# Two layers of a decoder trunk on one core: a ring of weight slots that gives the oldest, up panels with their pairs at other steps, and a third pair in two of them

## The chip, the core and the metric

The kernel runs on one core of a Trainium2 chip. The metric is the device time of one execution in microseconds. Weights come from HBM in every execution. TensorE (PE in the profile) multiplies, VectorE (DVE) and ScalarE (ACT) prepare its operands and take its results, SyncE (SP) and GpSimd (POOL) issue transfers.

## The reference

256 tokens of width 2048 pass through two layers: gated linear attention, then forgetting attention, each beside a cross attention into 256 memory tokens, and each followed by the same kind of channel mixer (FFN). All the change is in the FFN:

```python
def causal_dwconv(u, w, b):
    s_ = u.shape[1]
    up = jnp.pad(u, ((0, 0), (CONV_WIDTH - 1, 0), (0, 0)))
    return w[0] * up[:, 0:s_] + w[1] * up[:, 1:s_ + 1] + w[2] * up[:, 2:s_ + 2] + b

def conv_ffn(h, w_up, conv_w, conv_b, w_down):
    u = causal_dwconv(h @ w_up, conv_w, conv_b)
    a, val = split_cols(u, [FFN_HIDDEN, FFN_HIDDEN])
    return (jax.nn.silu(a) * val) @ w_down

# in each layer i, after the attention:
    h = rmsnorm(x, norm_ffn[i])
    x = x + conv_ffn(h, ffn_w_up[i], ffn_conv_w[i], ffn_conv_b[i], ffn_w_down[i])
```

FFN_HIDDEN is 5632, so w_up is 2048 x 11264 and w_down 5632 x 2048, all in float32.

## The kernel before

**Products.** A float32 operand is split into a high part in a rounded type and the low rest: `hi = cast(raw)` on ACT, `lo = raw - hi` on DVE. A product of two split operands is three products on PE: high with high, low with high, high with low. The activations `h` are split once. The weights are split as they come: one *unit* is 128 x 1024 elements (512 KB). SP loads it into a *raw slot* (L232), ACT casts it into a `whi` buffer (L242), DVE forms `wlo` (L243), and PE uses both (L421). There are five `whi` and five `wlo` buffers.

**The raw slots.** Five home slots (`RAWS`) serve the whole kernel. Each FFN adds two guests (the tile `raw2`) and drops them when it ends. `raw_slot` takes the next one by a counter modulo the number of slots. The guests' memory belonged to other tiles before: in both FFNs a load into a guest waits until the block `blk`, a transposed piece of the residual stream that the norm needs, has been written to its place in DRAM (`far`).

**Panels.** In each FFN 11 up panels of 16 units follow each other, numbered here 0 to 10 (`j // 4` in the code), with the parts of the down projection between them: panels 0 to 4, two down panels of 16 units, panels 5 to 7, two of 12 units, panels 8 to 10, and the last down panels. A *single* is one unit: 12 products of 512 columns. A *pair* is two units multiplied by a scheme with seven block products instead of eight (`pair_steps`): 21 products of 512 columns instead of 24. For it DVE forms differences of the two raw units in place (L446 to L449), there are four splits instead of two (w1 of half a unit, w2, w3, w4; L391 and L392), and the sums of the matching input blocks must be there (`usum`, made by `input_sums` and `token_sums`). w3 is cast from what L446 and L447 leave, w4 from what L448 and L449 leave. The products p1 to p7 and the singles go to eight PSUM banks; fast banks and slow banks change places from panel to panel (`flip`). When the last pair of a panel is done, `early` adds the banks p6, p7 and p5 on DVE (L1515 to L1518) into temporaries. When the last unit is done, `late` adds the banks p2, p4, p3 and x on DVE (L1524) and transposes the four results (L1475), which go through DRAM by POOL's transfers and come back for the convolution: taps on ACT (L1425), their sums (L1432), the gated product (L1445) and its split (L538), in DVE and ACT time of later panels.

**What sets the order.** A scheduler puts each engine's instructions into one queue at compile time, by the order of the code, priorities (`high_priority`) and `issue_after`; on the chip each queue runs in its order. The step at which a pair stands in a panel comes from `sums` and `ahead`: panels 0, 3 and 4 have one pair (units 6 and 7) at step 6; the panels of `MORE_IN` have two, units 6 and 7 at step 4 and units 11 and 12 at step 9. A step is one unit, so a pair takes two.

Of the kernel before, what the change touches and what calls it, by code (L numbers as in the profile page):

```python
# [34 lines left out]
SEVEN_UP = (6,)  # L35
# [2 lines left out]
MORE_IN = (1, 2, 5, 6, 7, 8, 9, 10)  # L38
SCRATCH = 4096
RAWS = 5  # L40


LEVELS = (64, 16, 4)
# [105 lines left out]
def _trunk(ctx: ExitStack, tc: tile.TileContext, xt, xtok, memt, wp, wgu, gns, gfin, cnv, par, msk, out):  # L149
# [36 lines left out]

    loads, casts, lows, ends, last_mm, sent = [], [], [], [], [], []
    home = rear.tile([P, RAWS * NUNIT], F32, name="raw")
    slots, taken = [home[:, i * NUNIT : (i + 1) * NUNIT] for i in range(RAWS)], [0]

    def raw_slot():

        taken[0] += 1
        return slots[taken[0] % len(slots)]
    scratch = [sm]
    parked = []

# [194 lines left out]
            lows.append(V.tensor_tensor(lo[:, :n], src, hi[:, :n].bitcast(F32), ALU.subtract))  # L392
        return hi, lo

    def pair_steps(units, src, sums, flip, pool, early, late, ahead=0):

        bank = {}
        fast, slow = ("p1", "p5", "p7", "p6"), ("p2", "p3", "p4", "x")
# [7 lines left out]
        plan = []  # L406
        at = 0
        while at < n:
            if at + ahead in sums:
                plan.append(at + ahead)  # L410
                at += 2
            else:
                plan.append(single.pop(0))
                at += 1
# [19 lines left out]
        for k in plan:  # L434
            if k in sums:
                with tc.high_priority(offset=AHEAD):
                    ra, rb = raw_slot(), raw_slot()
                    with tc.issue_after(loads[-1].ins):
                        for t, (off, _, w) in ((ra, units[k]), (rb, units[k + 1])):
                            loads.append(nc.sync.dma_start(t, wp[off : off + P * w].rearrange("(p n) -> p n", p=P)))  # L440
                st = [[sums[k][:, part, j, :] for part in range(2)] for j in (3, 0, 1, 2)]
                done = k == end[-1]
                w1 = split_more(ra[:, :512], 512)
                w2 = split_more(rb, 1024)
                with tc.high_priority(offset=AHEAD):
                    V.tensor_tensor(ra[:, :512], ra[:, 512:], ra[:, :512], ALU.subtract)  # L446
                    V.tensor_tensor(ra[:, 512:], rb[:, 512:], ra[:, 512:], ALU.subtract)  # L447
                    V.tensor_tensor(rb[:, 512:], rb[:, 512:], ra[:, :512], ALU.subtract)  # L448
                    summed = V.tensor_tensor(rb[:, :512], rb[:, :512], rb[:, 512:], ALU.subtract)  # L449
                three("p1", tok(k, 0), [t[:, :512] for t in w1], done)  # L450
                three("p2", tok(k + 1, 0), [t[:, :512] for t in w2])
                three("p3", st[3], [t[:, 512:] for t in w2])
                with tc.issue_after(summed.ins):
                    w3 = split_more(ra, 1024)
                three("p5", st[0], [t[:, :512] for t in w3], done)
                three("p7", st[2], [t[:, 512:] for t in w3], done)
                w4 = split_more(rb, 1024)
                three("p6", st[1], [t[:, 512:] for t in w4], done)
                last_mm.append(three("p4", tok(k + 1, 1), [t[:, :512] for t in w4]))
                if done:  # L460
                    with tc.issue_after(casts[-1].ins), tc.issue_after(lows[-1].ins):
                        early(bank)
                yield -1
                yield -1
                continue
            else:
                w = split_unit(units[k])
                last = k == n - 1
                steps = [(low, *place) for low in range(2) for place in places]
                if last:  # L470
                    steps.sort(key=lambda t: places.index(t[1:]))
                for low, name, b, h in steps:
                    for part in range(2 - low):
# [881 lines left out]
    def down_pair(l, p, f, src, sums, flip, pool, temps, then=None):  # L1355
# [17 lines left out]
            if then is not None:  # L1373
                then(f + h, b)

        return pair_steps(where["down", l, p, f], src, sums, flip, pool, early, late)

    def add_out(key, src, then=None, spare=None, last=None, first=0, hooks=None, late=1):

# [23 lines left out]
    def ffn(l, nx, h, m, ys, zs, landing, then, pool, temps, last=None, spare=None):  # L1403
        with tc.tile_pool(name=f"ffn{l}", bufs=1) as fp:
# [3 lines left out]
            up_sums = {k: held("usum", k) for k in (*SEVEN_UP, SEVEN_MORE)}  # L1408
            rooms = {i: held("dsum", i) for i in range(2)}
            guest = pool.tile([P, 2 * NUNIT], F32, name="raw2")  # L1410
            slots.extend(guest[:, i * NUNIT : (i + 1) * NUNIT] for i in range(2))
            cw = fp.tile([P, 4 * 88], F32, name="cw")
            nc.sync.dma_start(cw, cnv[l])
            taps = [fp.tile([P, 2, 2, T + i], F32, name=f"tap{i}") for i in range(3)]
# [41 lines left out]
            def input_sums(k):  # L1456

                r = fp.tile([P, 2, T], F32, name="cv", tag="cv")
                for s in range(2):
                    V.tensor_tensor(r[:, s, :], h[k + s][:, 0, :].bitcast(F32), h[k + s][:, 1, :].bitcast(F32), ALU.add)  # L1460
                token_sums(r, up_sums[k])


            def scale(b):
# [39 lines left out]
            def up_pair(j):  # L1504
# [17 lines left out]
                def late(b, h_, a):  # L1522
                    with tc.issue_after(turned_last[0].ins) if h_ and not b else nullcontext():
                        V.scalar_tensor_tensor(u[b, h_], a, scale(b), u[b, h_], ALU.mult, ALU.add)  # L1524
                    turns[h_](b, u[b, h_])

                return pair_steps(where["up", l, j], h, {k: up_sums[k] for k in (*SEVEN_UP, SEVEN_MORE)[: 1 + second]},
                                  count[2] % 2, pool, early, late, 2 * second)

            def first(k):  # L1530
                {2: lambda: nx.land(landing[0]), 3: nx.take, 8: nx.col,
# [7 lines left out]
                    tick(share if k >= 0 else 0.0)  # L1539

            def drive_up(j):
                drive(up_pair(j), 1.7 if j // 4 in MORE_IN else 1.45)

            for k in SEVEN_UP:
                input_sums(k)
# [50 lines left out]
            else:  # L1596
                hooks = {(2, 3): then.land, (2, 5): then.land, (2, 7): then.take, (3, 1): then.take, (3, 2): then.land,
                         (3, 5): then.take}
                for f, step, at in ((2, f2, 3), (3, f3, 0)):
                    for u in range(at, 8):  # L1600
                        step(u)
                        hooks.get((f, u), int)()
            del slots[RAWS:]

    def preparing(name, dst, pool, far, kept=None, tag="blk", queue=nc.sync):

# [204 lines left out]
```

## Time and profile before

| | |
|---|---|
| median of 3 runs | 2221.41 us (2220.82 to 2221.58) |
| the profiled execution | 2219.84 us |
| its span, first to last instruction | 2218.0 us |
| mean granted PE clock | 0.997 |
| PE, PEld, DVE, ACT busy | 99%, 83%, 82%, 65% of the span |
| second FFN's first product of L421 | 1502.39 us from the start |

PE is matrix multiplication, PEld its weight loads beside it, SPq the sequencer that issues transfers. A wait for several events is put down to the one that came last. An engine's waits matter where PE waits for them in the end. The rows shown below give start, length, engine, line, operation, written tile, read tiles and count, and in brackets how long the engine was idle ahead of it and what ended that.

### The profile page before, as it was taken

What the parts mean: (1) busy time and instruction counts of PE and PEld (TensorE: products, weight loads), DVE (VectorE), ACT (ScalarE), POOL (GpSimd) and SP (SyncE); (2) the same over time, 40 slices, a digit from 0 to 9 for tenths busy, and PEclk for the clock granted to TensorE, in tenths of its full rate; (3) what the DMA queues carried; (4) which work ended last, traced back from release to release, by engine and by line L of the source; (5) the groups of instructions that cost most, each with busy time, mean ns of one, the idle gap of its engine ahead of it and who ended that gap; (6) DMA issues with size and microseconds to landing.
All of it is one profiled execution on the core that took longest, in us unless ns stands there. A gap on an engine that the chain in (4) does not pass through costs nothing.

```text
span 2218.0 us, 30190 instructions
## 1 busy us (share of the span) xinstructions
PE 2196.9 (99%) x10285; PEld 1846.7 (83%) x10285; DVE 1828.6 (82%) x2715; ACT 1437.8 (65%) x2280; POOL 136.8 (6%) x257
## 2 busy tenths in 40 slices
PE   9999999999999999999999999999999999999998
PEld 7888888878888888888888998877888888888886
DVE  7768976679988889889987569668998888988996
ACT  6655655557887568647865555445788657765874
POOL 0000000001100000001010000000100000100000
PEclk9999999999999999999999999999999999999999
DMA  9766666776777667666877667666687667776683
GB/s 360 260 222 217 199 207 230 252 231 223 258 250 239 199 228 256 231 207 224 268 246 245 219 207 235 224 217 223 224 263 248 222 203 245 242 236 211 230 283 113
DMA packets 166291, 515.41 MB, mean 232 GB/s; under 512 B 20780, under 2 KB 42552, under 8 KB 166136
## 3 DMA queue, kind: packets, MB, share of 16 engines
q1 hardware_dynamic: 149064, 460.99, 63.2%
q0 software_dynamic: 16496, 51.71, 7.4%
q8 instruction: 80, 1.31, 0.2%
q10 hardware_dynamic: 576, 0.79, 0.1%
q14 instruction: 75, 0.61, 0.1%
HBM read 469.62 MB, written 43.79 MB: 231 GB/s over the span
## 4 chain that ended last, share of the span: by engine, by line
PE 96%; DVE 2%; ACT 1%; DMA 1%; issue 0%; SPq 0%; DVEq 0%; ACTq 0%
PE acc L421 29%; PE acc L347 26%; PE ps_s L421 15%; PE ps_o L421 7%; PE ps_t L421 7%; PE acc L273 3%; PE acc L318 3%; PE ps_s L347 2%; PE acc L377 2%; PE acc L271 1%; PE ps_s L1044 0%; DMA raw<-wp 0%; ACT whi L242 0%; PE ps_o L710 0%; PE ps_s L710 0%
## 5 line engine op out<-in xcount | busy, mean ns | idle before, releaser
L243 DVE TENSOR_TENSOR wlo<-raw,whi 128x1024 fp32r<-128x1024 f32 (+2 forms) x685 | 812.5, 1200 | 222.9 <-ACT whi L242 200.8
L242 ACT ACTIVATE whi<-raw 128x1024 fp32r<-128x1024 f32 (+2 forms) x685 | 704.3, 1045 | 347.8 <-PE acc L347 131.2
L347 PE MATMUL acc<-whi,B 128*128 128x512 f32 (+3 forms) x1248 | 290.9, 369 | 0.0
L391 ACT ACTIVATE whi<-raw 128x1024 fp32r<-128x1024 f32 (+1 forms) x184 | 173.7, 953 | 179.4 <-DVE raw L447 65.7
L347 PEld LDWEIGHTS acc<-whi,B 128*128 128x128 f32 x1248 | 226.8, 188 | 28.1
L392 DVE TENSOR_TENSOR wlo<-raw,whi 128x1024 fp32r<-128x1024 f32 (+1 forms) x184 | 198.3, 1084 | 26.8 <-ACT whi L391 23.8
L421 PE MATMUL acc<-whi,mix 128*128 128x512 f32 x746 | 191.7, 392 | 8.7 <-ACT whi L242 8.7
L421 PE MATMUL acc<-whi,B 128*128 128x512 f32 x720 | 186.9, 389 | 0.0
L421 PEld LDWEIGHTS acc<-whi,mix 128*128 128x128 f32 x746 | 141.2, 189 | 38.7 <-ACT whi L242 9.2
L347 PE MATMUL acc<-wlo,B 128*128 128x512 f32 (+3 forms) x624 | 159.1, 369 | 0.0
L421 PEld LDWEIGHTS acc<-whi,B 128*128 128x128 f32 x720 | 135.1, 188 | 28.5 <-ACT whi L242 0.5
L347 PEld LDWEIGHTS acc<-wlo,B 128*128 128x128 f32 x624 | 114.2, 188 | 14.6
L1425 ACT ACTIVATE tap<-yzu,cw 128x256 f32<-128x256 f32 x264 | 120.7, 534 | 5.4 <-DMA yzu<-far 5.4
L1425 ACT ACTIVATE tap<-fvt,cw 128x256 f32<-128x256 f32 x264 | 120.2, 530 | 3.1 <-DMA fvt<-far 3.1
L1432 DVE TENSOR_TENSOR tap<-tap,tap 128x1024 f32<-128x1024 f32 x88 | 106.7, 1213 | 9.0 <-ACT tap L1425 9.0
L421 PE MATMUL acc<-wlo,mix 128*128 128x512 f32 x373 | 105.0, 392 | 0.0
L421 PE MATMUL acc<-wlo,B 128*128 128x512 f32 x360 | 103.8, 389 | 0.0
L421 PE MATMUL ps_s<-whi,mix 128*128 128x512 f32 x374 | 103.8, 389 | 0.0
L421 PE MATMUL ps_s<-whi,B 128*128 128x512 f32 x324 | 89.9, 389 | 0.0
L421 PEld LDWEIGHTS acc<-wlo,mix 128*128 128x128 f32 x373 | 70.6, 189 | 14.8
L421 PEld LDWEIGHTS ps_s<-whi,mix 128*128 128x128 f32 x374 | 70.2, 188 | 14.6
L421 PEld LDWEIGHTS acc<-wlo,B 128*128 128x128 f32 x360 | 67.6, 188 | 14.0
(503 smaller groups left out, 3912.8 us busy)
## 6 DMA issues: line engine op xcount, KB each, us to landing
raw<-wp SPq DMA_DIRECT2D x741, 512.0 KB, 4.6
fvt<-far POOLq DMA_DIRECT2D x100, 128.0 KB, 5.2
raw<-wp SPq DMA_DIRECT2D x32, 384.0 KB, 3.4
far<-yu POOLq DMA_DIRECT2D x22, 512.0 KB, 3.0
far<-yzu POOLq DMA_DIRECT2D x22, 512.0 KB, 3.0
yzu<-far POOLq DMA_DIRECT2D x88, 128.0 KB, 4.8
raw<-wp SPq DMA_DIRECT2D x24, 388.0 KB, 3.5
x<-xtok SPq DMA_DIRECT2D x8, 512.0 KB, 7.0
```

What stands on the lines that cost most here:

```text
L242: casts.append(S.activation(hi[:, s], raw[:, s], AF.Copy))
L243: lows.append(V.tensor_tensor(lo[:, s], raw[:, s], hi[:, s].bitcast(F32), ALU.subtract))
L271: mm = TE.matmul(acc[p][c][:, :T], w[:, s], both[:, 0, :], start=False, stop=end and j == 3)
L273: mm = TE.matmul(acc[p][c], w[:, s], both, start=u == j == 0, stop=end and j == 3)
L318: mm = TE.matmul(acc[b][:, :n], src[kcs[j] - base][:, part, b * P : (b + 1) * P], w, start=u == 0 and low == part == j == 0, stop=u == end ...
L347: mm = TE.matmul(acc[b][:, :n], src[kc - base][:, part, b * P : (b + 1) * P], ready[low][:, j * room : j * room + n], start=i == low == pa ...
L377: mm = TE.matmul(acc[b][:, :n], src[kc - base][:, part, b * P : (b + 1) * P], w, start=i == low == part == j == 0, stop=i == end and low = ...
L391: casts.append(S.activation(hi[:, :n], src, AF.Copy))
L392: lows.append(V.tensor_tensor(lo[:, :n], src, hi[:, :n].bitcast(F32), ALU.subtract))
L421: r = TE.matmul(bank[name], x, w, start=name not in begun, stop=last)
L1425: S.activation(by_run(taps[i][:, s, c, i:]), zs[slot][:, :, 2 * c + s], AF.Copy if i else AF.Identity, bias=0.0 if i else w[3], scale=w[2 ...
L1432: V.tensor_tensor(taps[0], taps[0], taps[n][:, :, :, :T], ALU.add)
```

## The change

- The ring takes its oldest slot: `raw_slot` moves the first of the list to its end. The guests wait in `coming` and join the list's front at the first pair of the FFN; at the end of the FFN they are taken out.
- A table `UP_STEPS` tells at which step which pair stands. One pair: as before. Two pairs: steps 3 and 10 instead of 4 and 9. Three: steps 1, 6 and 11.
- Up panels 5 and 8 (`THIRD_IN`, the sixth and the ninth) have a third pair, units 13 and 14. The sums for it are made in that panel, after its first two steps, in the room of a `dsum` tile.
- `input_sums` issues behind the latest `lo` subtraction.

```diff
+UP_STEPS = ({6: 6}, {3: 6, 10: 11}, {1: 6, 6: 11, 11: 13})
+THIRD, THIRD_IN = 13, {5: 1, 8: 0}
...
-    slots, taken = [home[:, i * NUNIT : (i + 1) * NUNIT] for i in range(RAWS)], [0]
+    slots, coming = [home[:, i * NUNIT : (i + 1) * NUNIT] for i in range(RAWS)], []
...
-        taken[0] += 1
-        return slots[taken[0] % len(slots)]
+        slots.append(slots.pop(0))
+        return slots[-1]
...
-    def pair_steps(units, src, sums, flip, pool, early, late, ahead=0):
+    def pair_steps(units, src, sums, flip, pool, early, late, at_step):
...
-            if at + ahead in sums:
-                plan.append(at + ahead)
+            if at in at_step:
+                plan.append(at_step[at])
...
                 with tc.high_priority(offset=AHEAD):
+                    slots[:0] = coming
+                    del coming[:]
                     ra, rb = raw_slot(), raw_slot()
...
-            slots.extend(guest[:, i * NUNIT : (i + 1) * NUNIT] for i in range(2))
+            guests = [guest[:, i * NUNIT : (i + 1) * NUNIT] for i in range(2)]
+            coming.extend(guests)
...
-                for s in range(2):
-                    V.tensor_tensor(r[:, s, :], h[k + s][:, 0, :].bitcast(F32), h[k + s][:, 1, :].bitcast(F32), ALU.add)
-                token_sums(r, up_sums[k])
+                with tc.issue_after(lows[-1].ins) if lows else nullcontext():
+                    for s in range(2):
+                        V.tensor_tensor(r[:, s, :], h[k + s][:, 0, :].bitcast(F32), h[k + s][:, 1, :].bitcast(F32), ALU.add)
+                    token_sums(r, up_sums[k])
...
-                return pair_steps(where["up", l, j], h, {k: up_sums[k] for k in (*SEVEN_UP, SEVEN_MORE)[: 1 + second]},
-                                  count[2] % 2, pool, early, late, 2 * second)
+                more = second + (j // 4 in THIRD_IN)
+                return pair_steps(where["up", l, j], h, {k: up_sums[k] for k in UP_STEPS[more].values()},
+                                  count[2] % 2, pool, early, late, UP_STEPS[more])
...
             def drive_up(j):
-                drive(up_pair(j), 1.7 if j // 4 in MORE_IN else 1.45)
+                third = THIRD_IN.get(j // 4)
+                if third is not None:
+                    up_sums[THIRD] = held("dsum", third)
+                steps = up_pair(j)
+                if third is not None:
+                    for k in (0, 1):
+                        next(steps)
+                        tick(0.0)
+                    input_sums(THIRD)
+                drive(steps, 1.7 if j // 4 in MORE_IN else 1.45)
...
-            del slots[RAWS:]
+            slots[:] = [s for s in slots if not any(s is g for g in guests)]
```

The down panels pass `{k: k for k in sums}`, which leaves their pairs at the steps where they were. In the changed kernel the lines stand 2 to 16 further down: L234 is L232 of before, L245 is L243, L423 is L421, L444 is L440, L450 to L453 are L446 to L449, L394 is L392, L1481 is L1475, L1530 is L1524.

**SP, ahead of the second FFN.** `raw_130` are the home slots, `raw2` the guests, `blk` the blocks of the residual stream, `far` their place in DRAM, `yzu` where they come back. Before:

```order
L659 DMA far_13328<-blk_13314 128x1024
L232 DMA raw_130<-wp 128x1024
L664 DMA yzu_13525<-far_13328 32x4x256
L232 DMA raw_130<-wp 128x1024
L664 DMA yzu_13525<-far_13328 32x4x256 x3
L232 DMA raw_130<-wp 128x1024 x2
L659 DMA far_13503<-blk_13489 128x1024
L232 DMA raw2_13538<-wp 128x1024
L440 DMA raw2_13538<-wp 128x1024 x2
L232 DMA raw_130<-wp 128x1024 x2
```

and now:

```order
L663 DMA far_13366<-blk_13352 128x1024
L234 DMA raw_130<-wp 128x1024 x2
L668 DMA yzu_13563<-far_13366 32x4x256 x4
L234 DMA raw_130<-wp 128x1024 x7
L663 DMA far_13541<-blk_13527 128x1024
L444 DMA raw2_13576<-wp 128x1024 x2
```

Ahead of the second write to `far` stand nine loads where there were four, and the first load into a guest behind it is the pair's (L444) and no longer unit 0's (L232).

**PE, the second pair of panel 6.** `ps_t` is bank p6 of that pair, `acc` and `ps_s` other banks, `B8` to `B12` blocks of the input. Before:

```order
L421 MATMUL ps_t_7383<-whi_7485,usum_4429 128x512 x2
L421 MATMUL acc_7271<-whi_7485,B12_109 128x512 x2
L421 MATMUL ps_s_7371<-wlo_7476,usum_4429 128x512
L421 MATMUL ps_s_7375<-wlo_7476,usum_4429 128x512
L421 MATMUL acc_7268<-whi_7506,B9_106 128x512 x2
L421 MATMUL acc_7274<-whi_7506,B9_106 128x512 x2
L421 MATMUL acc_7277<-whi_7506,B9_106 128x512 x2
L421 MATMUL ps_t_7383<-wlo_7486,usum_4429 128x512
```

and now:

```order
L423 MATMUL ps_t_7385<-whi_7525,usum_4429 128x512 x2
L423 MATMUL acc_7290<-whi_7525,B12_109 128x512 x2
L423 MATMUL ps_s_7373<-wlo_7516,usum_4429 128x512
L423 MATMUL ps_s_7377<-wlo_7516,usum_4429 128x512
L423 MATMUL acc_7287<-whi_7546,B10_107 128x512 x2
L423 MATMUL acc_7293<-whi_7546,B10_107 128x512 x2
L423 MATMUL acc_7296<-whi_7546,B10_107 128x512 x2
L423 MATMUL ps_t_7385<-wlo_7526,usum_4429 128x512
```

The order within the pair is the same, and the single that PE begins between its parts is unit 10 now where it was unit 9: the last product of p6 (last row) was the 131st of the panel and is the 143rd. In the same way the first product with w4 of panel 7's first pair was that panel's 62nd and is its 50th.

**DVE, up to the last difference of panel 7's first pair.** `yu` takes the transposed results of panel 6, `cv` is the gated product. Before:

```order
L1475 STREAM_TRANSPOSE yu_4418<-temp_7495 128x16x32
L1524 SCALAR_TENSOR_TENSOR fvt_4412<-acc_7274,ny_4627,fvt_4412 128x512
L1475 STREAM_TRANSPOSE yu_4417<-temp_7496 128x16x32
L487 TENSOR_TENSOR cv_7561<-cv_7561 128x128
L446 TENSOR_TENSOR raw_130<-raw_130 128x512
L1475 STREAM_TRANSPOSE yu_4417<-fvt_4412 128x16x32
L488 TENSOR_TENSOR cv_7561<-cv_7561 128x128
L447 TENSOR_TENSOR raw_130<-raw_130 128x512
L448 TENSOR_TENSOR raw_130<-raw_130 128x512
L697 TENSOR_TENSOR dsum_7567<-cv_7561,dsum_7567 128x512
L449 TENSOR_TENSOR raw_130<-raw_130 128x512
```

and now:

```order
L1481 STREAM_TRANSPOSE yu_4418<-fvt_4412 128x16x32
L1481 STREAM_TRANSPOSE yu_4418<-temp_7535 128x16x32
L1530 SCALAR_TENSOR_TENSOR fvt_4412<-acc_7293,ny_4627,fvt_4412 128x512
L1481 STREAM_TRANSPOSE yu_4417<-temp_7536 128x16x32
L450 TENSOR_TENSOR raw2_4432<-raw2_4432 128x512
L701 TENSOR_TENSOR dsum_7569<-cv_7563,dsum_7569 128x512
L1481 STREAM_TRANSPOSE yu_4417<-fvt_4412 128x16x32
L451 TENSOR_TENSOR raw2_4432<-raw_130,raw2_4432 128x512
L1450 TENSOR_TENSOR cv_7717<-tap0_4435 128x512
L452 TENSOR_TENSOR raw_130<-raw_130,raw2_4432 128x512
L453 TENSOR_TENSOR raw_130<-raw_130 128x512
```

What DVE does for the end of panel 6 stands among the pair's differences in both. From the addition that reads bank p6 in panel 6 (L1515, now L1521) to the last difference stood 35 instructions, seven of them whole lows (L243), and now stand 33, five of them whole lows: two singles fewer lie between the two pairs. Between panels 9 and 10 it was 34 and is 32, between panels 1 and 2 31 and is 29.

More of the change, by code (lines that the diff above doesn't have):

```diff
@@ L1374, in late @@
                 then(f + h, b)
-        return pair_steps(where["down", l, p, f], src, sums, flip, pool, early, late)
+        return pair_steps(where["down", l, p, f], src, sums, flip, pool, early, late, {k: k for k in sums})
     def add_out(key, src, then=None, spare=None, last=None, first=0, hooks=None, late=1):
```

## The prediction

> **What bounds the kernel now.** I read the page's busy times first, then PE's waits, then the chain.
>
> ```profile
> span 2218.0 us, 30190 instructions
> PE 2196.9 (99%) x10285; PEld 1846.7 (83%) x10285; DVE 1828.6 (82%) x2715; ACT 1437.8 (65%) x2280; POOL 136.8 (6%) x257
> PE acc L421 <- ACT whi L242: 8.7, 1, 8.7
> PE ps_t L421 <- ACT whi L391: 0.9, 1, 0.9
> 543.52 10.88 PE acc L421 x48
> ```
>
> TensorE is the bound almost everywhere. 48 products of 512 columns take 10.88 us, so one costs 0.2267 us. Only two waits in the FFNs are over half a microsecond: 8.7 us once and 0.9 us once. A change therefore pays by taking products out, or by removing these waits, and it costs wherever PE begins to wait. So I looked at the 8.7 us, and then at how close VectorE (DVE) is to its limit in each panel.
>
> ```profile
> 1494.42 0.72 DVE blk L1637
> 1495.16 2.57 DMA far<-blk
> 1497.78 3.42 DMA raw<-wp
> 1501.28 1.06 ACT whi L242
> 1482.39 0.85 SPq L232 DMA_DIRECT2D raw<-wp  x2
> 1497.78 0.33 SPq L232 DMA_DIRECT2D raw<-wp  x1
> 1493.04 0.61 PE L347 MATMUL acc<-wlo,B 128*128 128x512 f32 x2
> 1502.39 3.78 PE L421 MATMUL acc<-whi,mix 128*128 128x512 f32 x8 [8.73 <-ACT whi L242]
> 1505.97 1.89 PE L421 MATMUL acc<-wlo,mix 128*128 128x512 f32 x4
> 1507.68 2.03 PE L421 MATMUL acc<-whi,mix 128*128 128x512 f32 x8
> 1493.00:1502.00 9.00, 0.66 (x3) 0.20 (x2) 2.75 (x5) 3.16 (x10) 0.00 (x0) 0.75 0.47 174
> 1502.00:1508.00 6.00, 5.61 (x14) 4.40 (x15) 5.63 (x5) 6.00 (x10) 0.00 (x0) 0.52 0.52 154
> ```
>
> The first four rows are the chain at the start of the second FFN. Its unit 0 goes into a guest slot, whose memory is that of the block `blk`. The load (1497.78) can start only when the transposed block has been written away (1495.16 + 2.57), and cast and product follow. The last column but two of the windows is the granted clock: the first 12 products after the wait run at about half rate. From 1493.04 to 1507.68 PE did 14 products, which take 3.2 us at 0.2267. **The hole costs 14.6 - 3.2 = 11.5 us.**
>
> ```profile
> 456.70:501.20 44.50, 43.55 (x191) 35.21 (x189) 35.13 (x65) 22.56 (x33) 0.00 (x0) 1.00 0.77 256
> 543.40:585.50 42.10, 42.10 (x187) 34.87 (x186) 39.98 (x49) 32.22 (x50) 5.47 (x10) 1.00 0.71 233
> 1590.00:1632.50 42.50, 42.44 (x187) 34.84 (x186) 40.63 (x48) 34.41 (x56) 5.50 (x10) 1.00 0.76 244
> 756.90:799.00 42.10, 42.10 (x187) 34.89 (x186) 32.85 (x37) 22.94 (x25) 0.00 (x0) 1.00 0.61 200
> 799.00:841.20 42.20, 42.20 (x188) 34.91 (x187) 37.59 (x45) 32.74 (x52) 5.51 (x10) 1.00 0.71 234
> 841.20:883.70 42.50, 42.46 (x187) 34.84 (x186) 42.08 (x54) 33.48 (x54) 5.50 (x10) 1.00 0.77 248
> 1032.60:1075.10 42.50, 42.50 (x188) 34.86 (x187) 42.14 (x54) 34.14 (x56) 5.51 (x10) 1.00 0.75 244
> 1888.20:1930.70 42.50, 42.44 (x187) 34.84 (x186) 42.03 (x54) 33.53 (x54) 5.52 (x10) 1.00 0.74 248
> 2079.70:2122.10 42.40, 42.40 (x187) 34.80 (x186) 42.05 (x54) 34.02 (x56) 5.51 (x10) 1.00 0.74 249
> ```
>
> Each row is one up panel (length, then PE, PEld, DVE, ACT): panel 0, panel 2 in both layers, panels 5, 6, 7 and 10, and panels 7 and 10 of layer 1. Numbers count from 0, so the panels that get a third pair are 5 and 8. A panel with two pairs is 186 products, 42.16 us. Panel 0 (189 products, 42.84 us) runs 1.7 us long. Panels 7 and 10 in both layers and panel 2 of layer 1 are about 0.3 us long, and there DVE is busy for 40.6 to 42.1 us of 42.5. In panel 5 DVE has over 9 us free.
>
> **The change part by part.**
>
> *Third pairs.* Each takes 3 products off: 2 layers x 2 panels x 3 x 0.2267 = **-2.7 us**. DVE pays for it: a pair has four splits instead of two, four differences, and its sums of the input.
>
> ```profile
> 1483.53 0.75 DVE L1460 TENSOR_TENSOR cv<-mix 128x256 f32<-128x256 f32 x2
> 1484.32 0.29 DVE L485 TENSOR_TENSOR cv<-cv 128x128 f32<-128x128 f32 x1
> 829.97 3.48 DVE L243 TENSOR_TENSOR wlo<-raw,whi 128x1024 fp32r<-128x1024 f32 x3
> 853.33 0.68 DVE L449 TENSOR_TENSOR raw<-raw 128x512 f32<-128x512 f32 x1
> ```
>
> The sums are 0.75 + 4 x 0.29 and one operation of 512 columns, 0.68 like L449 here: 2.6 us. The splits add 1.5 lows of 3.48 / 3 us, 1.7, and the differences 4 x 0.68, 2.7: 7.0 us in all. It lies in panel 5's free DVE time (32.9 + 7.0 = 39.9 of 41.5 us); ACT's 1.5 casts more, under 2 us, lie in 19 free ones. I take 0. If that cover were gone it would be like panel 7: 0.3 us, four times, 1.2 us.
>
> *Guests at the first pair.* Between the last two `far` writes ahead of the second FFN SP issues nine loads where it issued four, all for home slots. DVE and ACT split units 0 to 3 ahead of the last additions to x. `usum` still waits for the write on both, but behind it in their queues stand the pair's own splits now, and no longer unit 0's. The hole goes: **-11.5 us**. In layer 0 the same wait holds unit 5 and the pair behind it; that is panel 0's **-1.7 us**. Late next is the pair at step 6, whose two loads now wait for that write alone, in layer 1 behind five more loads. Bounds: 0, and panel 0's 1.7 us once more; I take **+0.5**, for one load fewer stands ahead of the pair.
>
> *Ring.* Oldest slot first is the order in which the old counter went round while nothing was added or removed. POOL has the same DMAs, a few of them moved. `input_sums` behind a low moves 2.5 us of DVE work that nothing waits for before step 6. Each 0.
>
> *Pairs farther apart.* The first pair moves from step 4 to 3, the second from 9 to 10. Inside a panel five singles lie between them instead of three, but from one panel's second pair to the next panel's first it is seven instead of nine. That seam is where DVE is full:
>
> ```profile
> 828.50 0.39 PE L421 MATMUL ps_t<-wlo,usum 128*128 128x512 f32 x1
> 829.37 0.68 DVE L1515 TENSOR_TENSOR fvt<-ps_t,fvt 128x512 f32<-128x512 f32 x1
> 854.11 1.06 ACT L391 ACTIVATE whi<-raw 128x1024 fp32r<-128x1024 f32 x1 [0.86 <-DVE raw L449]
> 854.12 1.83 PE L421 MATMUL acc<-whi,usum 128*128 128x512 f32 x6
> 1020.81 0.68 DVE L1515 TENSOR_TENSOR fvt<-acc,fvt 128x512 f32<-128x512 f32 x1
> 1044.72 0.68 DVE L449 TENSOR_TENSOR raw<-raw 128x512 f32<-128x512 f32 x1
> 541.09 0.39 PE L421 MATMUL ps_o<-wlo,B 128*128 128x512 f32 x1
> 541.52 0.75 DVE L1524 SCALAR_TENSOR_TENSOR fvt<-ps_o,ny,fvt 128x512 f32<-128x512 f32 x1 [0.98 <-PE ps_o L421]
> 554.87 0.69 DVE L449 TENSOR_TENSOR raw<-raw 128x512 f32<-128x512 f32 x1
> ```
>
> Panels 6 and 7: DVE's addition of bank p6 (L1515, 829.37) cannot run before p6's last product (828.50). From there DVE works without a gap to the pair's last difference (L449, shown above at 853.33, over at 853.94): 24.6 us. ACT casts it, and PE's first product with the result, the 62nd of the panel, starts at 855.23 where 855.03 was its turn; L449's end to that product is 1.3 us. Now p6's last product comes a step later, at 831.22. DVE reads a bank 0.4 us after its product (541.09, 541.52), so it goes on at 831.6. Between the two rows stand 33 instructions instead of 35, two whole lows fewer: 24.6 - 2.3 = 22.3 us, and the difference is over at 853.9 again. But PE now asks for the result 12 products, 2.72 us, earlier, at 852.3. Ready at 855.2: a wait of 2.9, with a slow product behind it **3.0 us**.
>
> Panels 9 and 10 in the same way: p6 is ready at 1023.1; the stretch 1020.81 to 1045.33 is 24.5 us, less two lows and a product (1445), plus a small add: 21.9. That gives 1045.0 + 1.3 = 1046.3 against PE's 1043.7: **2.6 us**. Panels 1 and 2: DVE waits for bank p2 in front of L1524; its last product now stands four products later, so it starts at 542.4. The stretch, 14.0 us, loses a low and a half and gains a small product: 12.6. 555.0 + 1.3 = 556.3 against 554.5: **1.9 us**. Each layer has these three: 2 x 7.5 = **+15.0 us**. They stand in the place of the old waits there, five of about 0.3: **-1.6 us**. The other first pairs follow panels in which DVE has 5 to 9 us free: 0.
>
> Bounds of this unknown wait: -1.6 us (all go, as the edit's words say, since a panel now gives DVE two more singles between its pairs) to 15 plus the slow clock below. I take the sum of rows, because the stretches of before come out by it within 0.3 us.
>
> *The sum* against the profiled execution (2219.84 us: the span 2218.0 and 1.8 around it): -2.7 - 11.5 - 1.7 + 0.5 - 1.6 + 15.0 = -2.0, so 2217.8 us. The median of the runs, 2221.4, stands 1.6 higher: **2219.4 us**.
>
> *The clock after a wait.* In the rows above, 8.7 us idle were followed by 5.3 us at half rate; the 0.9 us wait of panel 0 was followed by a granted clock of 1.00 over that panel. Waits of 1.9 to 3.0 us lie between; they are nearer to the second, and the sum takes no slow clock. [...]
>
> **The rivals.**
>
> *The waits at the seam stay small* (faster). DVE is in order here, but if it runs ahead of what I add up, only today's 1.6 us are left: 2219.4 - 13.4 = 2206.0; at half size 2212. For it: DVE is idle for 4.6 us in panel 6. Against: it goes into waiting for p6 (one step later now), after which 22 us of work stand in a row. It decides when the pair's last difference ends before 851.0 in panel 7's terms.
>
> *The clock falls in the waits* (slower): half rate for 5.3 us costs 2.6 us each. In panels 7 alone 2224.6; in all six 2219.4 + 15.4 = 2234.8. For it: six waits where there were two. Against: each is broken by four products, since w3 and w4 come one after the other. It decides somewhere between 0.9 and 8.7 us of idle PE; no row here is closer.
>
> *The hole of the second FFN doesn't go* but moves to the pair that now waits for the write: 2219.4 + 11.5 = 2230.9. Against: PE has six units, 16.3 us, to do meanwhile, and the write and load took 6.0.
>
> **How the numbers follow.** Forecast 0.48 (2216 to 2223). Small waits 0.30. Slow clock 0.12. Hole stays 0.06. The rest, 0.04: waits larger than summed. 0.2%, 4.4 us, is about what a measurement tells from no change: faster is below 2217.0, slower above 2225.8. Faster is 0.30 and 0.02 of the forecast's lower end; slower is 0.12 + 0.06 and half of the larger waits, 0.20; same is the rest of the forecast, 0.46, and the other half, 0.48. The range takes in small waits down to 2206 and the hole that stays, without the clock in all six: 2206 to 2231.
>
> **What would show it.** PE's count 12 lower; no wait of over 2 us at the start of the second FFN, and the granted clock 1.0 there; panel 0 near 42.9 us in both layers; panels 5 and 8 at 41.5 us with DVE near 39.9; PE waits on `whi` of a pair's third and fourth split early in panels 2, 7 and 10, six in all, 2 to 3 us each, those panels 44 to 45 us long. Wrong it would be if these six are missing or twice as long, if the clock falls there, or if the step-6 pair waits for its guests.

## The result and the profile after

The changed kernel takes 2234.26 us (median of 4 runs, 2230.25 to 2238.41) against 2221.11 us before on the same chip: ratio 1.0058, 95% interval 1.0042 to 1.0074. It is slower by 13.2 us, where 2219.4 was forecast, and the time lies above the range. The runs of before spread over 1.7 us, those of after over 8.

The profiled execution (2235.11 us) shows this on its page and in PE's waits (us in total, times, longest). L423 was L421, L393 was L391:

```profile
span 2233.3 us, 30275 instructions
PE 2201.8 (99%) x10273; PEld 1846.2 (83%) x10273; DVE 1848.6 (83%) x2767; ACT 1440.2 (64%) x2292; POOL 137.0 (6%) x257
PE ps_t L423 <- ACT whi L393: 10.6, 8, 3.5
PE acc L423 <- ACT whi L393: 5.9, 5, 2.1
PE ps_s L423 <- ACT whi L393: 3.2, 2, 1.6
```

PE has its 12 products fewer and the wait of 8.7 us is gone. In its place stand 15 waits on L393, the cast of a pair, 19.7 us in all. The windows by panel, as before the change (length, then PE, PEld, DVE, ACT, POOL busy; then the granted clock): panel 0; panel 2 in both layers; panel 5; panel 7 in both layers; panel 8; panel 10 in both layers; and the start of the second FFN, where the hole was (8.7 us of idle PE and a half-rate stretch behind it):

```profile
456.20:499.60 43.40, 43.23 (x191) 35.45 (x190) 35.43 (x66) 22.25 (x34) 0.00 (x0) 1.00 0.72 235
541.70:589.30 47.60, 44.11 (x187) 35.96 (x186) 43.32 (x55) 36.14 (x60) 5.50 (x10) 0.96 0.70 221
1592.90:1640.30 47.40, 44.02 (x187) 35.92 (x186) 42.86 (x54) 36.50 (x60) 5.50 (x10) 0.96 0.69 217
760.70:802.10 41.40, 41.40 (x184) 34.30 (x183) 38.36 (x49) 24.59 (x28) 0.00 (x0) 1.00 0.67 227
844.30:892.70 48.40, 45.59 (x188) 36.84 (x187) 42.78 (x54) 35.11 (x57) 5.51 (x10) 0.93 0.65 217
1895.30:1942.30 47.00, 44.17 (x188) 35.77 (x188) 42.81 (x54) 34.18 (x57) 5.52 (x10) 0.96 0.66 225
958.10:1001.10 43.00, 41.96 (x185) 34.20 (x184) 41.99 (x55) 25.01 (x29) 0.00 (x0) 1.00 0.65 218
1043.30:1088.20 44.90, 42.84 (x187) 34.63 (x186) 40.79 (x54) 32.54 (x54) 5.50 (x10) 1.00 0.74 226
2092.10:2137.10 45.00, 42.94 (x188) 34.69 (x187) 40.90 (x54) 32.67 (x54) 5.51 (x10) 1.00 0.73 232
1490.00:1507.00 17.00, 17.00 (x77) 14.08 (x76) 13.81 (x32) 9.69 (x15) 0.00 (x0) 1.00 0.94 329
```

Length less PE's busy time is idle PE: 3.5 and 3.4 us in panel 2, 2.8 and 2.8 in panel 7, 2.1 and 2.1 in panel 10, 1.0 in panel 8. In panels 2 and 7 that is not all: their clock is 0.93 to 0.96, and PE is busy for 44.0 to 45.6 us with 42.16 us of products. Windows over the slow stretches alone, panels 2 and 7 of the first layer, then of the second:

```profile
557.30:560.90 3.60, 3.60 (x10) 2.81 (x9) 3.60 (x4) 3.60 (x5) 2.31 (x5) 0.53 0.98 246
859.30:864.80 5.50, 5.50 (x15) 4.31 (x14) 5.50 (x5) 5.50 (x9) 1.64 (x3) 0.51 0.80 245
1608.80:1612.20 3.40, 3.40 (x10) 2.63 (x9) 3.40 (x4) 3.38 (x4) 2.17 (x4) 0.50 1.02 274
1910.30:1912.80 2.50, 2.50 (x8) 1.94 (x7) 2.50 (x4) 2.50 (x4) 1.70 (x4) 0.55 0.89 244
```

The granted clock falls to half at 557.48, 857.85, 1608.79 and 1909.16 us, each time 1.0 to 1.4 us after the end of a wait. From product to product these stretches lose 1.6, 2.5, 1.6 and 1.1 us against 0.2267 us each: 6.8 us. In the timeline of the first layer, an addition of taps in panel 1 (the first row), the wait of panel 2 (the next seven) and the waits of panel 7 (the last two), with an engine's idle time in brackets; L1437 was L1432, and L1430, which scales the taps, was L1425:

```profile
527.80 1.23 DVE L1437 TENSOR_TENSOR tap<-tap,tap 128x1024 f32<-128x1024 f32 x1 [3.86 <-ACT tap L1430]
542.76 0.75 DVE L1530 SCALAR_TENSOR_TENSOR fvt<-ps_o,ny,fvt 128x512 f32<-128x512 f32 x1
544.09 0.69 DVE L450 TENSOR_TENSOR raw<-raw 128x512 f32<-128x512 f32 x1
547.09 0.68 DVE L451 TENSOR_TENSOR raw<-raw,raw 128x512 f32<-128x512 f32 x1
553.06 0.68 DVE L452 TENSOR_TENSOR raw<-raw,raw 128x512 f32<-128x512 f32 x1
554.60 0.68 DVE L453 TENSOR_TENSOR raw<-raw 128x512 f32<-128x512 f32 x1
555.37 1.06 ACT L393 ACTIVATE whi<-raw 128x1024 fp32r<-128x1024 f32 x1 [1.47 <-DVE raw L453]
556.48 0.73 PE L423 MATMUL ps_t<-whi,usum 128*128 128x512 f32 x2 [3.49 <-ACT whi L393]
856.73 1.21 PE L423 MATMUL acc<-whi,usum 128*128 128x512 f32 x4 [2.07 <-ACT whi L393]
858.69 1.22 PE L423 MATMUL acc<-whi,usum 128*128 128x512 f32 x2 [0.74 <-ACT whi L393]
```

The four differences of panel 2's pair (L450 to L453) are spread over 11 us of DVE's order. The last ends at 555.28, its cast follows, and PE stands from 552.99 on. That DVE, and no load, is late is seen from the rows between: DVE has no idle time in them. It had none since 527.80, in panel 1, where it had waited 3.86 us for ACT's scaled taps.

### The profile page after: what moved, and what is told of

It is laid out like the page before. It is cut to its first block, busy times and chain, and to the rows that moved or that the text cites. A ratio compares the mean times of both kernels' runs of the same rounds, so it can differ in the third digit from the quotient of the medians.

```text
span 2233.3 us, 30275 instructions
## 1 busy us (share of the span) xinstructions
PE 2201.8 (99%) x10273; PEld 1846.2 (83%) x10273; DVE 1848.6 (83%) x2767; ACT 1440.2 (64%) x2292; POOL 137.0 (6%) x257
## 4 chain that ended last, share of the span: by engine, by line
PE 91%; DVE 5%; DMA 2%; ACT 1%; issue 1%; POOL 0%; SPq 0%; DVEq 0%; ACTq 0%
PE acc L349 26%; PE acc L423 25%; PE ps_s L423 14%; PE ps_o L423 7%; PE ps_t L423 6%; PE acc L275 3%; PE acc L320 3%; PE ps_s L349 2%; PE acc L379 2%; PE acc L273 1%; DVE wlo L394 1%; DMA raw<-wp 1%; ACT whi L393 1%; DVE x L511 1%; DMA far<-blk 0%
## 5 line engine op out<-in xcount | busy, mean ns | idle before, releaser
L245 DVE TENSOR_TENSOR wlo<-raw,whi 128x1024 fp32r<-128x1024 f32 (+2 forms) x677 | 804.1, 1204 | 186.4 <-ACT whi L244 169.6
L244 ACT ACTIVATE whi<-raw 128x1024 fp32r<-128x1024 f32 (+2 forms) x677 | 691.8, 1043 | 307.6 <-PE acc L349 141.9
L393 ACT ACTIVATE whi<-raw 128x512 fp32r<-128x512 f32 x200 | 188.8, 953 | 250.5 <-DVE raw L451 109.1
L394 DVE TENSOR_TENSOR wlo<-raw,whi 128x512 fp32r<-128x512 f32 x200 | 216.7, 1088 | 27.7 <-ACT whi L393 21.8
L423 PE MATMUL acc<-whi,mix 128*128 128x512 f32 x746 | 193.2, 391 | 0.0
L423 PE MATMUL acc<-whi,B 128*128 128x512 f32 x710 | 185.8, 391 | 0.0
L423 PEld LDWEIGHTS acc<-whi,mix 128*128 128x128 f32 x746 | 140.9, 189 | 29.6
L423 PEld LDWEIGHTS acc<-whi,B 128*128 128x128 f32 x710 | 134.1, 189 | 28.2
L1437 DVE TENSOR_TENSOR tap<-tap,tap 128x1024 f32<-128x1024 f32 x88 | 107.4, 1220 | 48.0 <-ACT tap L1430 48.0
L1430 ACT ACTIVATE tap<-fvt,cw 128x256 f32<-128x256 f32 x264 | 120.5, 532 | 6.9 <-DMA fvt<-far 6.6
L1430 ACT ACTIVATE tap<-yzu,cw 128x256 f32<-128x256 f32 x264 | 120.6, 532 | 6.7 <-DMA yzu<-far 6.5
L423 PE MATMUL acc<-wlo,mix 128*128 128x512 f32 x373 | 105.5, 389 | 0.0
L423 PE MATMUL ps_s<-whi,mix 128*128 128x512 f32 x374 | 105.1, 390 | 0.0
L423 PE MATMUL acc<-wlo,B 128*128 128x512 f32 x355 | 102.2, 389 | 0.0
L423 PE MATMUL ps_s<-whi,B 128*128 128x512 f32 x318 | 89.7, 392 | 0.0
L423 PEld LDWEIGHTS ps_s<-whi,mix 128*128 128x128 f32 x374 | 70.5, 188 | 14.8
L423 PEld LDWEIGHTS acc<-wlo,mix 128*128 128x128 f32 x373 | 70.1, 188 | 14.6
L423 PEld LDWEIGHTS acc<-wlo,B 128*128 128x128 f32 x355 | 66.6, 188 | 13.9
```

The costliest lines, as they stand in the source:

```text
L244: casts.append(S.activation(hi[:, s], raw[:, s], AF.Copy))
L245: lows.append(V.tensor_tensor(lo[:, s], raw[:, s], hi[:, s].bitcast(F32), ALU.subtract))
L393: casts.append(S.activation(hi[:, :n], src, AF.Copy))
L423: r = TE.matmul(bank[name], x, w, start=name not in begun, stop=last)
L1430: S.activation(by_run(taps[i][:, s, c, i:]), zs[slot][:, :, 2 * c + s], AF.Copy if i else AF.Identity, bias=0.0 if i else w[3], scale=w[2 ...
L1437: V.tensor_tensor(taps[0], taps[0], taps[n][:, :, :, :T], ALU.add)
```

## The experiments

**Spacing back, ring and third pairs kept.**

```diff
-UP_STEPS = ({6: 6}, {3: 6, 10: 11}, {1: 6, 6: 11, 11: 13})
+UP_STEPS = ({6: 6}, {4: 6, 9: 11}, {1: 6, 6: 11, 11: 13})
```

> The ring and the third pairs as in the changed kernel; in the panels with two pairs the pairs stand at the old steps (4 and 9). Spacing theory (the wider spacing makes the waits of panels 2, 7 and 10, and the clock falls in them): panels 2, 7 and 10 go back to 42.2 to 42.5 us each from 47.6, 47.5, 48.4, 46.9, 45.0 and 45.0, 25.6 us in all, so about 2234.3 - 25.6 = 2208.7 us, with no half-rate record. Rival (the waits come from the ring's new order, which gives the pairs other slots, or from the third pairs): panels 2, 7 and 10 keep waits of 2 us and more, and the time stays above 2225. Panel 8: if its 1.0 us wait is work put off from panel 7's seam, the panel is 41.5 us and the time nearer 2206; if it is the third pair's own, 42.9 us.

Measured: 2205.34 us against 2220.6 before, ratio 0.9928 (0.9914 to 0.9941). That is the median of five executions; one of them took 4914.8 us, which nothing on record explains, and the other four 2204.2 to 2205.9. Panels 2, 7, 8 and 10 of the first layer:

```profile
542.10:584.20 42.10, 42.10 (x187) 34.89 (x186) 39.92 (x49) 31.93 (x49) 5.47 (x10) 1.00 0.76 241
839.20:881.40 42.20, 42.20 (x187) 34.92 (x187) 41.75 (x54) 33.12 (x54) 5.51 (x10) 1.00 0.74 244
946.00:987.50 41.50, 41.50 (x185) 34.36 (x184) 39.30 (x49) 25.90 (x29) 0.00 (x0) 1.00 0.68 228
1029.60:1071.80 42.20, 42.20 (x187) 34.92 (x187) 41.70 (x54) 33.70 (x55) 5.50 (x10) 1.00 0.76 245
```

No idle PE and no fall of the clock, and the same in the second layer. So the spacing costs 28.9 us (2234.26 to 2205.34, measured on two occasions whose times before differ by 0.5 us), and the rest of the change brings 15.3. This kernel beats both others. Panel 8 is at its 41.5 us, with DVE busy for 39.3 instead of 42.0. The two down panels ahead of it, first in the changed kernel, then here, show where the 2.7 us come from:

```profile
892.70:925.30 32.60, 32.60 (x145) 26.99 (x144) 20.66 (x24) 16.86 (x26) 5.47 (x10) 1.00 0.77 255
925.30:958.10 32.80, 32.53 (x142) 26.31 (x141) 32.68 (x41) 22.45 (x35) 0.00 (x0) 1.00 0.60 197
881.40:914.00 32.60, 32.60 (x145) 27.02 (x144) 24.38 (x29) 22.85 (x40) 5.47 (x10) 1.00 0.75 240
914.00:946.00 32.00, 32.00 (x142) 26.47 (x142) 31.60 (x42) 18.48 (x26) 0.00 (x0) 1.00 0.60 202
```

Over the two down panels and panel 8 DVE has the same work in both: 20.66 + 32.68 + 41.99 = 95.3 and 24.38 + 31.60 + 39.30 = 95.3 us. With the wide spacing 3.7 us less of it is done in the first down panel, where DVE has room; 1.1 us of that come in the second and 2.7 us in panel 8.

**The ring alone.** The same, and no third pairs:

```diff
-THIRD, THIRD_IN = 13, {5: 1, 8: 0}
+THIRD, THIRD_IN = 13, {}
```

> The ring alone: old steps, no third pair in panels 5 and 8. Spacing theory: the hole at the second FFN (11.5 us) and the excess of panel 0 (3.0 us in both layers, by the traces) go, nothing else: 2221.1 - 11.5 - 3.0 = 2206.6 us. Against the run with the third pairs (old steps too): if the third pairs bring their 12 products, that one is 2.7 us faster than this; if panel 8's waits eat it, the two are within 0.5 us. Rival (the ring's order itself costs): above 2215 us.

Measured: 2209.68 us, ratio 0.9949 (0.9937 to 0.9962): 10.9 us less than before, 3.1 us above what was expected, and 4.3 us more than with the third pairs. These bring more than their 2.7 us of products, since without them the old waits of about 0.3 us in panels 7 and 10 stand in the trace again, 1.3 us in both layers. Why the third pairs take them away I haven't tried. The profiled execution of this kernel (2211.1 us, the slowest of its five) also has two waits, 2.3 us together, in panel 2 of the second layer, with ten tap scalings of ACT queued ahead of a pair's cast; the first of them starts at 1599.07 us, after 3.63 us of idle ACT that ended when its data came back from DRAM.

**One half of the spacing at a time.** Only the second pair later:

```diff
-UP_STEPS = ({6: 6}, {3: 6, 10: 11}, {1: 6, 6: 11, 11: 13})
+UP_STEPS = ({6: 6}, {4: 6, 10: 11}, {1: 6, 6: 11, 11: 13})
```

> As the changed kernel, but in panels with two pairs the first pair stands at its old step (4), the second at the new one (10). If each of the two moves brings half of the lateness (2.7 us a step), the waits shrink to 3.5 + 0.3 - 2.7 = 1.1 us in panel 2, about 0.4 in panel 7, none in panel 10, too short for the clock: old steps + 3 us, about 2212 us. If the earlier first pair alone is the cause, the time is that of the old steps, 2209. If the later second pair alone is it (its late bank moves the add that the next panel's pair stands behind), the waits stay whole and the time is that of the changed kernel, 2228 to 2235.

Only the first pair earlier:

```diff
-UP_STEPS = ({6: 6}, {3: 6, 10: 11}, {1: 6, 6: 11, 11: 13})
+UP_STEPS = ({6: 6}, {3: 6, 9: 11}, {1: 6, 6: 11, 11: 13})
```

> As the changed kernel, but with the second pair at its old step (9) and only the first pair at the new one (3). Halves: as with the second pair alone, about 2212 us. If the earlier first pair alone is the cause: 2228 to 2235 us, with the waits of panels 2, 7 and 10 whole. If the later second pair alone is the cause: 2209 us.

Measured: 2211.60 us (ratio 0.9958, 0.9945 to 0.9972) and 2217.23 us (0.9983, 0.9974 to 0.9992). PE's longest kinds of wait between 500 and 2140 us, first with the second pair late, then with the first pair early:

```profile
PE ps_s L423 <- ACT whi L393: 1.5, 1, 1.5
PE ps_t L423 <- ACT whi L393: 4.1, 6, 1.3
PE acc L423 <- ACT whi L393: 2.4, 2, 1.2
```

Against the old steps the halves cost 6.3 and 11.9 us, 18.2 together, and both at once 28.9. Neither is the cause alone. Even halves were expected, about 2212 us for each run; the earlier first pair costs about twice as much as the later second one. With either half no wait is longer than 1.5 us, and neither trace has a half-rate stretch in its FFNs (the mean granted clock is 0.999 in both); that accounts for 6.8 of the 10.7 us by which both exceed the sum of the halves. The interval of the changed kernel's time is 3.6 us to either side, so the 10.7 are rough.

**The waits filled.** The changed kernel with products into a bank that the next product starts anew:

```diff
+FILL = {(l, p): f for l in (0, 1) for p, f in ((2, {"p6": 14}), (7, {"p5": 9, "p6": 3}))}
...
+        def cover(name, x, w):
+            for _ in range(fill.pop(name, 0)):
+                mm(name, x[0], w, True)
+                begun.discard(name)
...
+                cover("p5", tok(k, 0), w2[0][:, :512])
                 three("p5", st[0], [t[:, :512] for t in w3], done)
...
+                cover("p6", tok(k, 0), w3[0][:, :512])
                 three("p6", st[1], [t[:, 512:] for t in w4], done)
```

> The changed kernel with products whose result is thrown away put into the waits of the first pair of panels 2 and 7: 14 before p6's in panel 2 (3.2 us, the wait was 3.5), 9 before p5's (2.0 us, was 2.1) and 3 before p6's (0.7 us, was 0.7) in panel 7, in both layers. No wait gets shorter: the panels' end is set by the same differences. Clock theory (the half-rate spells at 557, 859, 1609 and 1910 us, 9, 13, 8 and 6 products or 8.2 us together, come from TensorE's idle time just before them): no half-rate spell there, 2234.3 - 8.2 = 2226 us, and the runs spread over 2 to 3 us instead of 8. Rival (they come by themselves, or from the load): they stay, 2230 to 2238 us. If the products delay anything (the weights' buffers are held up to 3 us longer), the time would be above 2238.

Measured: 2227.51 us (ratio 1.0028, 1.0018 to 1.0039), 6.8 us less than the changed kernel, for 52 products more. Panels 2 and 7 of the first layer and panel 7 of the second:

```profile
542.40:587.70 45.30, 45.30 (x201) 37.51 (x200) 41.34 (x53) 34.55 (x57) 5.52 (x10) 1.00 0.71 228
842.70:888.30 45.60, 45.49 (x200) 37.02 (x199) 43.23 (x55) 33.91 (x56) 5.53 (x10) 1.00 0.72 231
1889.00:1934.90 45.90, 45.52 (x199) 37.01 (x199) 43.59 (x55) 35.50 (x58) 5.55 (x10) 1.00 0.70 229
```

The clock is 1.00 in all of them, and in panel 2 of the second layer, and 0.999 over the whole span; the trace has no half-rate stretch in the FFNs. So the four of the changed kernel came from the idle time. As a measure of their size the run is rougher than it looks: the intervals of the two kernels leave the 6.8 us open by about 4. The products also shift a part of DVE's order (a few rows in a hundred); panel 8's wait is gone here too, and panel 2 of the second layer keeps one of 1.0 us. Seven of the eight runs lie in 2224.1 to 2228.8, one at 2232.6.

**The waits filled in part.** The same `cover` with fewer products:

```diff
+FILL = {(0, 2): {"p6": 3}, (1, 2): {"p6": 6}, (0, 7): {"p5": 3}, (1, 7): {"p6": 3}}
```

> The same with only part of each wait filled: panel 2 keeps about 2.8 us of idle TensorE in the first layer (3 products put in) and 2.1 in the second (6); panel 7 keeps 1.4 + 0.7 in the first (3 before p5's) and 2.1 + 0.05 in the second (3 before p6's). If the clock falls only after more than about 2.6 us within some 4 us of time (it didn't after 1.4 + 1.1 and 1.6 + 0.6 in earlier runs, and did after 2.2 + 0.9): at most one half-rate spell, in panel 2 of the first layer, so 2226 to 2228 us. If what is idle lowers it in proportion: about half of the 8.2 us, 2230 us. If idle time isn't the cause: 2234 us.

Measured: 2230.47 us (ratio 1.0041, 1.0028 to 1.0055). PE's first products after the waits, then the windows of the same panels, each in order of time: panel 2, panel 7, and both again in the second layer (L425 and L394 were L423 and L393).

```profile
557.06 1.12 PE L425 MATMUL ps_t<-whi,usum 128*128 128x512 f32 x2 [2.46 <-ACT whi L394]
857.27 1.20 PE L425 MATMUL acc<-whi,usum 128*128 128x512 f32 x4 [1.40 <-ACT whi L394]
859.22 0.73 PE L425 MATMUL acc<-whi,usum 128*128 128x512 f32 x2 [0.76 <-ACT whi L394]
1605.96 0.73 PE L425 MATMUL ps_t<-whi,usum 128*128 128x512 f32 x2 [2.01 <-ACT whi L394]
1905.14 1.83 PE L425 MATMUL acc<-whi,usum 128*128 128x512 f32 x4 [2.08 <-ACT whi L394]
542.70:589.80 47.10, 44.64 (x190) 36.49 (x189) 42.88 (x55) 35.73 (x59) 5.50 (x10) 0.96 0.71 222
844.80:890.40 45.60, 43.44 (x190) 35.32 (x189) 41.61 (x54) 32.66 (x53) 5.52 (x10) 1.00 0.71 226
1591.30:1637.20 45.90, 43.89 (x194) 35.98 (x193) 41.24 (x52) 35.16 (x59) 5.50 (x10) 1.00 0.69 219
1892.70:1939.50 46.80, 44.72 (x190) 36.57 (x189) 42.93 (x55) 34.02 (x56) 5.53 (x10) 0.96 0.69 224
```

The clock fell after 2.46 us and after 2.08, and did not after 2.01 or after 1.40 + 0.76. The expectation of one fall at most was wrong. Half of the stretches are left, and half of the 6.8 us. What sets the wait of 2.01 us apart from that of 2.08 is seen when the time is divided every 3.41 us, at the times at which the granted clock of this trace changes. Two such windows hold the wait of 2.01 us, one holds that of 2.08:

```profile
1601.68:1605.09 3.41, 2.27 (x11) 1.54 (x9) 3.41 (x7) 0.96 (x3) 0.94 (x2) 1.00 0.37 154
1605.09:1608.50 3.41, 2.54 (x11) 2.12 (x12) 3.41 (x5) 3.41 (x4) 2.66 (x6) 1.00 0.83 249
1902.05:1905.46 3.41, 1.33 (x6) 0.80 (x5) 3.38 (x7) 1.44 (x3) 1.31 (x3) 1.00 0.49 202
```

Idle PE is 1.14, 0.87 and 2.08 us in them. Behind the last, from 1905.46 to 1908.87, the clock is at half: the five products from 1906.76 on start 0.43 us apart, against 0.2267.

**The spacing on the kernel before.** Old ring, no third pairs, two pairs at steps 3 and 10:

```diff
+UP_STEPS = ({6: 6}, {3: 6, 10: 11})
...
-            if at + ahead in sums:
-                plan.append(at + ahead)
+            if at in at_step:
+                plan.append(at_step[at])
...
```

> The kernel before with the new steps of two pairs (3 and 10) alone: the old ring, no third pairs. Spacing theory: the hole of 11.5 us stays, and panels 2, 7 and 10 get what they got in the changed kernel, which is 2234.3 - 2205.3 = 29 us less the 3.0 us of panel 8: 2220.6 + 26 = 2247 us, clock falls included (2238 if there are none). Rival (the spacing is harmless without the new ring or the third pairs): 2221 to 2226 us.

Measured: 2247.62 us (2239.98 to 2248.47), ratio 1.0111 (1.0096 to 1.0126). The hole's wait, and panels 7 and 10 of the first layer (L422 and L243 were L421 and L242):

```profile
PE acc L422 <- ACT whi L243: 8.7, 1, 8.7
847.00:895.20 48.20, 45.62 (x188) 36.81 (x187) 43.10 (x55) 36.09 (x59) 5.51 (x10) 0.93 0.67 218
1044.30:1090.90 46.60, 44.35 (x188) 35.91 (x186) 42.44 (x55) 33.71 (x55) 5.50 (x10) 0.96 0.72 225
```

The spacing costs 27 us without the ring and the third pairs as well. The clock fell in panel 10 here, where it had stayed up in the changed kernel: the waits there are 1.61 + 0.44 us, and here 1.81 + 0.44.

**Less work ahead of the differences.** The changed kernel with `add_tap` empty, which leaves out the additions of the convolution's taps, so that the output is another one:

```diff
-                with tc.issue_after(lows[-1].ins):
-                    V.tensor_tensor(taps[0], taps[0], taps[n][:, :, :, :T], ALU.add)
+                return
```

> The changed kernel without the additions of the convolution's taps on VectorE (the output is then that of one tap in three; 88 rows of 1.2 us, 107 us of VectorE in all; one or two of them lie ahead of the late differences in each of panels 2, 7 and 10). Queue theory (the pair's differences are late because of the rows that stand ahead of them in VectorE's order, not because of their loads or slots): each wait loses at least 2.4 us in panel 2, 2.3 to 2.4 in panels 7 and 10, so all six shrink below 1.2 us, the clock stays up, panel 8's 1.2 us goes too: 2204 to 2209 us. Rival (load or slots): the waits stay over 2 us, above 2225.

Measured: 2213.97 us, ratio 0.9968 (0.9956 to 0.9981). The time is above the 2204 to 2209 us expected. Panels 7, 8 and 10 did as the queue theory has it: their idle time goes to 0.6, 0 and 0.4 us. Panel 2 did not: it keeps 1.5 + 0.3 us in the first layer, and 2.3 + 0.3 in the second, with a half-rate stretch. Its two longest waits, and the panel in the second layer:

```profile
PE ps_s L423 <- ACT whi L393: 3.8, 2, 2.3
1580.10:1627.40 47.30, 44.58 (x187) 35.81 (x186) 41.14 (x54) 38.39 (x63) 5.47 (x10) 0.96 0.74 239
```

In panel 2 the four differences are now one block that begins later (551.1 us in the first layer, 544.1 in the changed kernel): DVE's order is another one, so the row count ahead isn't the only thing that changed. The run speaks for the queue and against the loads, but it doesn't price panel 2.

## Why the prediction was wrong

Against the profiled spans the change costs 2233.3 - 2218.0 = 15.3 us, where the sum had -2.0. By the prediction's steps:

- *The clock after a wait* is the step that failed most: "the sum takes no slow clock". The traces have 6.8 us of half rate, in panels 2 and 7 of both layers. I had two rows, 0.9 us without a fall and 8.7 us with one, and took the nearer. A row between was missing, and with it 2 to 3.5 us was a range in which I knew nothing. The clock fell behind 2.07 to 2.41 us of idle PE within 3.41 us in the changed kernel, and behind 2.08 in the partly filled one. The rival "the clock falls in the waits" gave 2224.6 to 2234.8 and had 0.12; it is what happened, in four of its six places. Its price of 2.6 us each was too high; it measured 1.1 to 2.5. That its upper end lies beside the measured time is luck: 15.4 us of clock stand there for 6.8, and the rest came from the steps below.
- *Panels 7 and 10*: +3.0 and +2.6 us each. Idle PE measured 2.8 and 2.1. The mechanism, one step later for bank p6 and one earlier for the product that waits, was right, and the halves show that both steps count.
- *Panel 2*: +1.9, measured 3.5 and 3.4. The term took DVE to wait for bank p2 and to start on L1530 1.0 us before the panel. The row at 542.76 shows it 1.0 us into the panel, which begins at 541.7, and with no idle time ahead of it: DVE was behind already. The stretch from there to the last difference, 12.5 us, is the 12.6 that was summed. What failed is the wait that it starts from. DVE last stood idle not for a bank but for ACT's scaled taps in panel 1, until 527.80 (3.86 us, and 4.25 in the second layer); from there to the last difference it is not idle again in the first layer, and for 0.6 us in the second. In panels 7 and 10 it does stand idle for p6, 0.45 to 2.2 us ahead of L1521 (L1515 before), as was summed. Why the taps came late in panel 1 no run separates. This lateness and the 0.3 to 0.9 us that PE loses in each panel beyond the waits themselves make the six 20.5 us long without the half rate, against 15.0.
- *Third pairs at 0*: right in panel 5 (41.4 us; DVE 38.4 where 39.9 was summed, so the 7.0 us of a pair are 5.5). Wrong in panel 8, 1.5 us long in both layers, 3.0 in all: the work that the seam of panel 7 puts off was left out. The same work makes the second down panel ahead of it 0.8 us long in the first layer, 1.0 in both.
- *Hole*: -11.5, confirmed; PE is busy throughout from 1490 to 1507 at clock 1.00. *Panel 0*: both layers together are 1.4 us over their products, where -1.7 and +0.5 left 0.5. *Products*: -2.7, confirmed by the count. *Old waits*: -1.6, right in size, but the reason was wrong. They were to go because the new waits stand in their place; they are gone too with the old steps and the third pairs, where there are no new ones.

6.8 for the clock, 5.5 for the six waits, 3.0 for panel 8, 1.0 for the down panels and 0.9 for panel 0 make 17.2 of the 17.3 us between -2.0 and 15.3. Without the 15.0 us of the spacing the sum is -17.0, or 2204.4 us, and that kernel measured 2205.3. The prediction itself gave 2206.0 for that case, since there it kept the old waits.

## What to carry to other kernels

On an engine that is 99% busy in program order, a step that is moved on both sides of a seam takes slack from two places at once: count the lateness from the last point where the feeding engine was idle, whatever it waited for there, not from the nearest read of a bank, and look where the work that it pushes off will land. In the changed kernel's FFNs a half-rate stretch that lost 1.1 to 2.5 us stood behind each wait of TensorE of 2.07 us or more, and none behind panel 10's of 1.61 and 1.63: where a wait may come to that length, add such a stretch to its price, or fill the wait. When a change bundles several edits, sum them apart: here one edit lost 28.9 us and hid the 15.3 that the others won.

## What the runs showed of the hardware

All that follows is read from the profiled executions and the run times of this case and holds for them. In the changed kernel's FFNs the granted clock is at half rate from 557.48 to 560.89, 857.85 to 864.68, 1608.79 to 1612.20 and 1909.16 to 1912.57 us: for 3.41 us or twice that, and the later falls come 88, 308 and 396 times 3.413 us after the first. In the kernel before it is at half rate from 1497.47 to 1507.71 us, three times 3.41. Counted from the first instruction, these times lie 1.11 us past a multiple of 3.413 us in the changed kernel, 2.43 in the kernel before, and 0.82 in the partly filled one. The windows of 3.41 us ahead of the four falls in the changed kernel, and last the one of panel 10 behind which the clock stayed up:

```profile
554.07:557.48 3.41, 1.00 (x4) 0.86 (x5) 3.41 (x6) 2.11 (x3) 2.77 (x5) 1.00 0.42 162
854.44:857.85 3.41, 1.34 (x5) 0.67 (x4) 3.38 (x6) 1.95 (x4) 2.59 (x5) 1.00 0.42 168
1605.38:1608.79 3.41, 1.30 (x6) 1.06 (x7) 3.41 (x5) 2.41 (x3) 2.77 (x5) 1.00 0.51 181
1905.74:1909.16 3.42, 1.20 (x4) 0.67 (x4) 3.39 (x6) 2.21 (x4) 2.29 (x5) 1.00 0.41 163
1052.41:1055.83 3.42, 1.80 (x9) 1.18 (x8) 3.42 (x10) 1.14 (x2) 2.08 (x4) 1.00 0.47 192
```

Idle PE is 2.41, 2.07, 2.11 and 2.22 us ahead of the falls, and 1.62 in the last. With the traces of before and after divided in this way, from 20 us on, seven windows at full clock hold 2.07 to 3.41 us of idle PE, and half rate follows each; no other holds more than 1.64 us, and half rate follows none. The partly filled kernel agrees: 2.08 us in one window stood ahead of a fall, and 2.01 us in two, as 1.14 + 0.87, did not. Between 1.64 and 2.07 us these windows show nothing; with the spacing alone the clock fell in panel 10 of both layers (0.96 over the panel) with waits of 1.81 + 0.44 and 1.82 + 0.30 us. In the changed kernel half rate went on for a second window behind one with 0.74 us of idle PE (857.85 to 861.27), and ended behind one with 0.57 (1909.16 to 1912.57).

Whether these times also lie elsewhere in each run of one kernel isn't shown. If they do, the same wait can lower the clock in one run and not in the next, and this may be why the two kernels with the full spacing whose waits are longest spread over 8 us from run to run. The mean granted clock that the record has for every run fits: in the changed kernel it is 0.996 for 2230.25 us, 0.995 for 2233.40 and 2235.11, and 0.993 for 2238.41; with the spacing alone 0.995 for 2239.98, and 0.990 to 0.994 for the three runs at 2247.5 to 2248.5. There is one trace for each kernel, so which falls make the difference isn't shown. The filled kernel has a run 3.7 us above its others at a clock of 0.998, so the clock isn't all of it.
